# Low parts of weight units made by a transfer that adds, in the attention of a two-layer trunk

## The chip, the core and the metric

The kernel runs on one core of a Trainium2 chip. A core has TensorE (matrix products into the PSUM banks), VectorE, ScalarE and GpSimd (elementwise work), SyncE (here only a queue for transfers), an on-chip memory SBUF of 128 partitions, and 16 DMA engines that carry transfers between HBM and SBUF. Each engine works through its own queue in order and waits on semaphores. The metric is the device time of one execution, in microseconds, as the median of several runs.

## What is computed

The reference is a decoder trunk with two layers on 512 positions of width 1024, in float32. Layer 0 mixes tokens by a gated MLP, layer 1 by attention with 16 heads of 64, each followed by a gated MLP with a causal convolution of three taps. The change lies in the attention:

```python
proj = h @ w_qkvf
q, k, v, f_logit = jnp.split(proj, [D_MODEL, 2 * D_MODEL, 3 * D_MODEL], axis=-1)
log_f = jax.nn.log_sigmoid((f_logit + b_f).astype(jnp.float32))
cum = jnp.cumsum(log_f, axis=1).transpose(0, 2, 1)
...
logits = logits + cum[:, :, q0:q1, None] - cum[:, :, None, :q1]
p = jax.nn.softmax(jnp.where(mask, logits, neg), axis=-1)
o = jnp.einsum("bhqk,bkhd->bqhd", p, vb)      # per block of 128 queries
return o @ w_o
```

## The kernel before

All weights are cut into 176 units of 128x1024 float32 (512 KB), used once each, in order. `fetch` (line 75) brings in one unit: SyncE issues its transfer to a `raw` buffer (three of them), ScalarE casts `raw` to the high part `whi`, rounded to the type TensorE takes at speed, and VectorE subtracts that from `raw` to make the low part `wlo` (`split`, line 110). `whi` and `wlo` have two buffers each, so the cast for unit n+1 waits until TensorE is through with unit n-1. `unit` (line 85) fetches one unit ahead of the one that it returns. Each product is three matmuls (`triple`, line 164): L167 high by high, L168, and L169. Where the weight is the stationary operand, as in the attention's products, L167 and L168 read `whi` and only L169 reads `wlo`.

The attention (`fox`, line 363) first makes v (units 96 to 103), then q and k, two units for each pair of heads (units 104 to 119), and the output product (units 120 to 127; the first three of them are first halves of three groups of outputs, 120 to 122). The products of q, k and the output come from a generator that is woven with the attention proper: 20 triples run first, and then each of 71 slots takes two triples and one step of `attend`. A unit has eight triples, so it lasts four slots, one head. In a slot, `logits` (line 561) makes the logits of one block of queries, of 128 to 512 columns, in one of two PSUM banks `s` by three matmuls (L572 to L574), takes the row maximum on VectorE (L576), the exponential on ScalarE (L578), and normalises on VectorE (L579, L580). `turn` (line 582) transposes the probabilities of an earlier slot (L590) and splits them in two (`hl`, by `split`), and `values` (line 596) multiplies them by v (L602, L603). After the last triple of q or k, `stack_q` and `stack_k` scale the product and split it into the stacked operands of the logits (L528 to L534, L540 to L546), on VectorE and ScalarE; one cast of each is on GpSimd, and it issues no transfers.

The kernel names the engine of every instruction, but not its place in the queue: the framework plans the order of each queue from dependences, the order in which the kernel is written, and estimated durations. It may put an instruction ahead of one that is written earlier.

Of the kernel before, what the change touches and what calls it, by code (L numbers as in the profile page):

```python
# [8 lines left out]
F32 = mybir.dt.float32  # L9
F32R = mybir.dt.float32r  # L10
BF16 = mybir.dt.bfloat16
I32 = mybir.dt.int32
AF = mybir.ActivationFunctionType
ALU = mybir.AluOpType
# [28 lines left out]
class Trunk:  # L43
# [28 lines left out]
        return self.ps(tag)  # L72


    def fetch(self):
        nc = self.nc
        raw = self.sb("raw", 3, [P, 1024])
        nc.sync.dma_start(out=raw, in_=self.ins["w"][self.iu])
        self.iu += 1
        hi = self.sb("whi", 2, [P, 1024], F32R)  # L80
        lo = self.sb("wlo", 2, [P, 1024], F32R)
        self.split(hi, lo, raw)
        self.ahead.append((hi, lo))

    def unit(self, depth=2):
# [752 lines left out]
```

## Time and profile before

| | us |
|---|---|
| median of 3 runs (1090.64 to 1091.21) | 1091.2 |
| the profiled execution | 1091.33 |
| its span, first to last instruction | 1089.6 |
| TensorE busy | 1074.4 (99%) |
| VectorE busy | 622.1 (57%) |
| ScalarE busy | 441.5 (41%) |
| GpSimd busy | 70.4 (6%) |

The profile shows one execution. Busy time on TensorE includes overlap of matmuls in flight, so 99% doesn't say that it works at its best rate; its waits are read from the distance between starts of instructions. The products of q, k and the output, with the attention slots between them, lie between 605 and about 807 us of the span. The granted clock of TensorE is 0.994 of full speed over the whole.

### The profile page before, as it was taken

Reading aid. Unit: us, or ns where it says so; the run is one execution under the profiler, and the core shown is the slowest. Engines: PE = TensorE matmul, PEld = TensorE weight load, DVE = VectorE, ACT = ScalarE, POOL = GpSimd, SP = SyncE. Lnnn points to the kernel's source line nnn. Section 1 sums busy time; section 2 is a strip of 40 time slices with the busy share of each in tenths; the row PEclk is TensorE's granted clock in tenths of the full one; section 3 lists DMA queues with packets and bytes.
Section 4 is the critical chain, followed back from the end, with each engine's and each line's share of the span. In section 5 each row is a group of like instructions: output and inputs, shape, how many; then the busy total and the mean of one; then the engine's idle time right before and its main releaser. Section 6 shows DMA issues by size and latency. Waiting matters only on the chain.

```text
span 1089.6 us, 12928 instructions
## 1 busy us (share of the span) xinstructions
PE 1074.4 (99%) x5018; PEld 885.5 (81%) x5018; DVE 622.1 (57%) x1007; ACT 441.5 (41%) x706; POOL 70.4 (6%) x62
## 2 busy tenths in 40 slices
PE   8999999999999999999999999999989999999997
PEld 7878888888888888888887888877768888888886
DVE  5535856534555665545254699999564655655242
ACT  6332333322333433333133577777442433433232
POOL 5000000001200000001020010110030000000000
PEclk9999999999999999999999999999989999999999
DMA  6222222222223222222222211111122223232222
GB/s 257 96 79 96 93 82 78 96 98 96 98 78 97 97 97 97 99 96 98 97 96 83 98 61 41 60 62 59 59 78 97 95 97 98 78 116 78 97 97 78
DMA packets 28669, 99.44 MB, mean 91 GB/s; under 512 B 3456, under 2 KB 3712, under 8 KB 28608
## 3 DMA queue, kind: packets, MB, share of 16 engines
q1 hardware_dynamic: 27744, 96.42, 25.7%
q10 hardware_dynamic: 864, 2.20, 0.5%
q8 instruction: 39, 0.64, 0.2%
q14 instruction: 22, 0.18, 0.1%
HBM read 96.12 MB, written 2.10 MB: 90 GB/s over the span
## 4 chain that ended last, share of the span: by engine, by line
PE 89%; DVE 7%; ACT 2%; DMA 1%; issue 1%; ACTq 0%; DVEq 0%
PE psg L167 11%; PE psg L168 11%; PE psg L169 11%; PE pss L169 9%; PE pss L167 9%; PE pss L168 9%; PE psa L167 4%; PE psa L168 4%; PE psa L169 4%; PE psb L167 4%; PE psb L168 4%; PE psb L169 4%; DVE wlo L113 2%; DVE hl L113 1%; DVE z L545 1%; PE psa L590 1%
## 5 line engine op out<-in xcount | busy, mean ns | idle before, releaser
L113 DVE TENSOR_TENSOR wlo<-raw,whi 128x1024 fp32r<-128x1024 f32 (+1 forms) x173 | 219.6, 1269 | 371.4 <-ACT whi L112 359.2
L112 ACT CAST whi<-raw 128x1024 fp32r<-128x1024 f32 (+1 forms) x173 | 180.8, 1045 | 453.0 <-PE psg L168 132.2
L167 PE MATMUL psg<-x,whi 128*128 128x512 f32 x336 | 136.1, 405 | 0.0
L169 PE MATMUL psg<-x,wlo 128*128 128x512 f32 x336 | 131.3, 391 | 0.0
L168 PE MATMUL psg<-x,whi 128*128 128x512 f32 x336 | 130.9, 390 | 0.0
L167 PE MATMUL pss<-x,whi 128*128 128x512 f32 x192 | 75.9, 395 | 0.0
L168 PE MATMUL pss<-x,whi 128*128 128x512 f32 x192 | 74.7, 389 | 0.0
L169 PE MATMUL pss<-x,wlo 128*128 128x512 f32 x192 | 74.7, 389 | 0.0
L169 PEld LDWEIGHTS psg<-x,wlo 128*128 128x128 f32 x336 | 63.1, 188 | 13.5
L167 PEld LDWEIGHTS psg<-x,whi 128*128 128x128 f32 x336 | 63.9, 190 | 11.1
L141 POOL TENSOR_TENSOR tmp<-tmp,tmp 128x512 f32<-128x512 f32 x28 | 47.0, 1678 | 399.8 <-ACT tmp L140 398.5
L168 PEld LDWEIGHTS psg<-x,whi 128*128 128x128 f32 x336 | 63.3, 188 | 11.2
L167 PE MATMUL psg<-z,whi 128*128 128x512 f32 x128 | 50.3, 394 | 0.6 <-ACT z L112 0.6
L169 PE MATMUL psg<-z,wlo 128*128 128x512 f32 x128 | 50.0, 391 | 0.0
L168 PE MATMUL psg<-z,whi 128*128 128x512 f32 x128 | 49.8, 389 | 0.0
L169 PE MATMUL pss<-z,wlo 128*128 128x512 f32 x112 | 44.8, 402 | 3.7 <-DVE wlo L113 3.7
L167 PE MATMUL psa<-x,whi 128*128 128x512 f32 x120 | 47.3, 394 | 0.0
L169 PE MATMUL psa<-x,wlo 128*128 128x512 f32 x120 | 46.7, 389 | 0.0
L168 PE MATMUL psa<-x,whi 128*128 128x512 f32 x120 | 46.7, 389 | 0.0
L167 PE MATMUL psb<-x,whi 128*128 128x512 f32 x120 | 46.7, 389 | 0.0
L169 PE MATMUL psb<-x,wlo 128*128 128x512 f32 x120 | 46.7, 389 | 0.0
L168 PE MATMUL psb<-x,whi 128*128 128x512 f32 x120 | 46.7, 389 | 0.0
(282 smaller groups left out, 2221.7 us busy)
## 6 DMA issues: line engine op xcount, KB each, us to landing
raw<-w SPq DMA_DIRECT2D x175, 512.0 KB
out<-v SPq DMA_DIRECT2D x8, 256.0 KB
h<-x ACTq DMA_DIRECT2D x3, 512.0 KB
raw<-w SPq DMA_DIRECT2D x2, 256.0 KB
h<-x ACTq DMA_DIRECT2D x2, 256.0 KB
pt<-ws SPq DMA_DIRECT2D x1, 512.0 KB
pt<-bs SPq DMA_DIRECT2D x1, 512.0 KB
z<-cum SPq DMA_DIRECT2D x32, 8.0 KB
```

The source lines that it names most:

```text
L112: nc.scalar.copy(out=hi, in_=src)
L113: nc.vector.tensor_tensor(out=lo, in0=src, in1=hi.bitcast(F32), op=ALU.subtract)
L141: nc.gpsimd.tensor_tensor(out=self.acc, in0=self.acc, in1=sq, op=ALU.add)
L167: self.nc.tensor.matmul(out, ah, bh, start=start, stop=False)
L168: self.nc.tensor.matmul(out, ah, bl, start=False, stop=False)
L169: self.nc.tensor.matmul(out, al, bh, start=False, stop=stop)
L545: nc.vector.tensor_tensor(out=bk[0:HD], in0=f[own], in1=ak[own].bitcast(F32), op=ALU.subtract)
L590: nc.tensor.transpose(pt[:, (qi - kb) * P : (qi - kb + 1) * P], pr[:, o : o + P], self.ident)
```

## The change

Only `fetch` is changed. For units 106 to 122 (the units of q and k from the second pair of heads on, and the first three of the output product) VectorE's subtraction is gone. In its place ScalarE writes the negated high part into `lo`, and GpSimd issues a transfer that reads the unit again from HBM and adds it onto what stands in `lo`: `lo` becomes the unit less its high part. All other units are split as before.

```diff
+    ADDED = range(106, 123)
+
     def fetch(self):
         nc = self.nc
         raw = self.sb("raw", 3, [P, 1024])
         nc.sync.dma_start(out=raw, in_=self.ins["w"][self.iu])
-        self.iu += 1
         hi = self.sb("whi", 2, [P, 1024], F32R)
         lo = self.sb("wlo", 2, [P, 1024], F32R)
-        self.split(hi, lo, raw)
+        if self.iu in self.ADDED:
+            nc.scalar.copy(out=hi, in_=raw)
+            nc.scalar.activation(out=lo, in_=hi.bitcast(F32), func=AF.Copy, scale=-1.0)
+            nc.gpsimd.dma_start(out=lo, in_=self.ins["w"][self.iu].bitcast(F32R), accum_op=ALU.add)
+        else:
+            self.split(hi, lo, raw)
+        self.iu += 1
         self.ahead.append((hi, lo))
```

## Rows read from the trace of the kernel before

**Rows 1.** The page, busy us, share of the span and count, by engine.
```profile
PE 1074.4 (99%) x5018; PEld 885.5 (81%) x5018; DVE 622.1 (57%) x1007; ACT 441.5 (41%) x706; POOL 70.4 (6%) x62
```

**Rows 2.** Windows: stretch, its length, busy us by engine, clock, DMA share, GB/s.
```profile
680.00:700.00 20.00, 19.79 (x111) 16.05 (x110) 18.91 (x44) 15.07 (x37) 2.23 (x2) 1.00 0.17 55
...
780.00:800.00 20.00, 15.70 (x65) 11.25 (x64) 12.80 (x16) 10.42 (x17) 4.53 (x3) 0.92 0.13 45
```

**Rows 3.** TensorE in order of time: start, us, engine, line, operation [idle before].
```profile
692.97 0.38 PE L590 MATMUL psa<-ident,pt 128*128 128x128 f32 x2
693.56 0.50 PE L572 MATMUL pss<-z,z 128*128 128x512 f32 x1 [0.21 <-ACT pt L578]
...
699.30 0.40 PE L169 MATMUL psg<-x,wlo 128*128 128x512 f32 x1
...
703.08 0.38 PE L590 MATMUL psa<-ident,pt 128*128 128x128 f32 x2
703.22 0.48 PE L572 MATMUL pss<-z,z 128*128 128x512 f32 x1
```

**Rows 4.** Waits, 620 to 800 us: us in total, times, longest.
```profile
PEld pss L572 <- ACT pt L578: 3.4, 8, 0.5
```

**Rows 5.** The chain that ended last, 600 to 820 us: start, us, what.
```profile
649.05 1.67 DVE wlo L113
...
688.72 1.21 DVE wlo L113
...
692.57 0.34 DVE sm L576
692.94 0.57 ACT pt L578 x2
```

**Rows 6.** The tile raw, 600 to 800 us: count, duration ns min/median/max.
```profile
L112 ACT CAST whi<-raw x23: 1027/1048/1056, 599.8 to 797.4; 128x1024 fp32r<-128x1024 f32 x23
L113 DVE TENSOR_TENSOR wlo<-raw,whi x22: 1212/1225/2296, 600.9 to 795.5; 128x1024 fp32r<-128x1024 f32 x22
```

**Rows 7.** ScalarE in order of time, from 687 us.
```profile
687.61 1.05 ACT L112 CAST whi<-raw 128x1024 fp32r<-128x1024 f32 x1 [0.67 <-PE psg L168]
...
688.92 0.61 ACT L544 CAST z<-tmp 64x512 fp32r<-64x512 f32 x1
...
692.05 0.48 ACT L112 CAST hl<-psa 128x384 fp32r<-128x384 f32 x1
692.94 0.47 ACT L578 ACTIVATE pt<-pss,sm 128x256 f32<-128x256 f32 x1 [0.41 <-DVE sm L576]
```

**Rows 8.** SyncE's queue in order of time, one issue of a unit.
```profile
700.57 0.33 SPq L78 DMA_DIRECT2D raw<-w  x1
```

**Rows 9.** Windows of 0.5 us behind that issue, first and last with data.
```profile
701.50:702.00 0.50, 0.50 (x4) 0.41 (x3) 0.50 (x2) 0.18 (x1) 0.00 (x0) 1.00 0.88 221
...
703.00:703.50 0.50, 0.50 (x5) 0.41 (x3) 0.50 (x2) 0.35 (x1) 0.00 (x0) 1.00 0.24 90
```

**Rows 10.** GpSimd in order of time, two casts of one size.
```profile
649.03 0.61 POOL L546 CAST z<-tmp 64x512 fp32r<-64x512 f32 x1 [3.58 <-DVE tmp L540]
...
688.78 1.61 POOL L546 CAST z<-tmp 64x512 fp32r<-64x512 f32 x1 [4.16 <-DVE tmp L540]
```

**Rows 11.** ScalarE in order of time, casts of units 106 and 107.
```profile
610.43 1.05 ACT L112 CAST whi<-raw 128x1024 fp32r<-128x1024 f32 x1 [3.58 <-PE psg L168]
...
615.91 1.05 ACT L112 CAST whi<-raw 128x1024 fp32r<-128x1024 f32 x1
```

**Rows 12.** TensorE in order of time: first reads of wlo, units 106, 107, 125.
```profile
616.35 0.39 PE L169 MATMUL psg<-x,wlo 128*128 128x512 f32 x1
...
622.49 0.39 PE L169 MATMUL psg<-x,wlo 128*128 128x512 f32 x1
...
797.84 0.80 PE L169 MATMUL pss<-z,wlo 128*128 128x512 f32 x1 [3.68 <-DVE wlo L113]
```

**Rows 13.** VectorE in order of time, the widest normalisation.
```profile
697.70 0.48 DVE L580 TENSOR_SCALAR pt<-pt,sm 128x512 f32<-128x512 f32 x1
```

## The prediction, on record before the change was run

> **What bounds the kernel now.** I read five views, from coarse to fine. The page's busy times come first: TensorE is busy in 1074.4 of 1089.6 us, VectorE in 622.1 and ScalarE in 441.5 [rows 1]. So only what makes TensorE wait can be won, and the averages of the other engines say nothing until they are cut by stage. The windows by stage do that: in the attention VectorE is busy in 18.91 of 20 us, ScalarE in 15.07, GpSimd in 2.23, and the DMA engines are used to 0.17; in the last stretch before the next layer TensorE is busy in only 15.70 of 20 [rows 2]. The reader is to see there that VectorE, idle in nearly half of the whole span, is almost full just where the change takes work from it. Whether TensorE pays for that is seen in the order of its instructions. Between the two transposes and the 512-wide logits of a slot there are 0.59 us at 692.97, but 0.14 us at 703.08, one unit later [rows 3]. The same two steps without a wait are worth 0.14, so this wait costs 0.45 us. In the waits of the stretch from 620 to 800 us, that line's weight load waits for the exponential 8 times, 3.4 us in all [rows 4]; six of the eight are the 0.45 kind, one for each pair of heads in the steady part. The chain of waits says what is behind it: the subtraction that makes `wlo` at 688.72, then VectorE's queue up to the row maximum at 692.57, the exponential at 692.94, and TensorE at 693.56 [rows 5]. The logits may not start until the exponential has emptied the bank used two slots before.
>
> So attention is bound by TensorE with a small loss, 3.4 us, that VectorE's queue causes. That is the most the change can win at the place where it acts, 0.3% of the time.
>
> **The change part by part.** *Removed:* 17 subtractions on VectorE, 1.225 us each [rows 6], 20.8 us; two of them per 20 us bring VectorE from 18.9 to 16.5. None lies on TensorE itself. At 688.72 the subtraction stands in front of the maximum that the stalled logits wait for; with it gone that maximum can be done up to 1.2 us sooner, more than the 0.45 us that TensorE waits. Bounds: 0 (another link holds the exponential) and 3.4 us; I take 3.4, since 1.2 is well over 0.45.
>
> *Added on ScalarE:* 17 negations of 128x1024. The trace has no such operation; the nearest row is the cast of the same size on the same engine, 1.048 us [rows 6]. That is 17.8 us, and 15.07 becomes 17.2 of 20 us. ScalarE has room on average, but not everywhere: from the cast of `whi` at 687.61 it runs without a gap to 692.53 (the last cast starts at 692.05 and takes 0.48) [rows 7], and the exponential starts 0.41 us after that. A negation right behind `whi` would push the exponential to about 693.5, 0.55 us later than now. The order on a queue is not the order in which the kernel is written: `whi` is written behind the casts of `k`, and runs ahead of them (the first is at 688.92). A planner orders by what it takes to be ready. With VectorE free at 688.7 the maximum is ready early, so I expect its exponential to be put ahead of the casts of the next slot, and the negation into the gaps. I count 0, with bounds of 0 and +0.55 us per pair.
>
> *Added on GpSimd and the DMA engines:* 17 transfers of 512 KB that read the unit a second time and add. Nothing in the trace adds in flight, so I bound it. Below: the plain transfer of the same unit is issued at 700.57; data moves from 701.5 to 703.1, which is 2.6 us from issue to the last byte, 1.6 of it data [rows 8, 9]. Above: four times the data time, and an issue on GpSimd as long as that engine's longest cast, 1.61 us [rows 10]: 0.95 + 6.4 + 1.6 = 9.0 us. I take twice the data time, since both operands must be read, and a short issue of 0.6: 0.95 + 3.2 + 0.6 = 4.75 us. A sentence apart: the Trainium skill ("DMA: Bandwidth & Descriptors", section on the anatomy of one DMA on the gpsimd path) gives 2.0 us and the bytes over 436 GB/s, by which an estimate for this transfer is 3.2 us, 4.4 if the bytes count twice; no row here shows it.
>
> What this wait covers: `whi` starts at 687.61 [rows 7], and the first matmul that reads the new `lo` is at 699.30 [rows 3], 11.7 us later. Take off the cast and the negation, 1.05 each: 9.6 us are left if the negation is prompt. If it is put behind ScalarE's run without gaps (3.9 us later, less the 0.5 saved by what it no longer pushes), 6.2 are left. 4.75 fits both; 9.0 fits the first alone. Behind the issue on GpSimd's queue stand only the two casts per pair of heads, which feed logits of the next pair: they have many us.
>
> *The first units.* Unit 106 is fetched before attention slots stretch the units. Its `whi` starts at 610.43 [rows 11] and TensorE wants `lo` at 616.35 [rows 12]: 5.9 us, less 2.1 for cast and negation, leaves 3.8. With 4.75 TensorE waits 0.95 us; by the bounds 0 to 5.2. The `whi` of unit 107 starts at 615.91 and its `lo` is wanted at 622.49, 0.95 later by then: 6.6 + 0.95 - 2.1 = 5.4, so no second wait; with 9.0 the first wait has already moved it. From unit 108 on the slots give the time above.
>
> *At nothing:* the raw buffer comes free after the cast instead of after the subtraction, so SyncE's next transfer starts about 1.2 us sooner and may overlap the adding one; with the DMA engines at 0.17, and two more transfers of some 3.2 us in 20, they stay near half used. The wait of 3.68 us at 797.84 [rows 12], with the low clock behind it, is for unit 125, whose `lo` VectorE still makes: 0 either way, unless the planner's order there shifts.
>
> *A rule against the change.* In this trace GpSimd and VectorE slow each other: the cast of `ak` takes 1.61 us at 688.78, beside `wlo`, and 0.61 at 649.03 [rows 10], where instead `wlo` took 1.67 [rows 5] against 1.225. The Trainium skill ("SBUF — State Buffer", section "Who interferes with whom") says that VectorE in its two-port modes (the normalisation's kind of instruction can enter them) and GpSimd lock each other out of a shared port pair, whoever issues first, and that descriptor generation on GpSimd needs it. The trace agrees for casts; none shows it for a transfer. What a hold between the two would cost, from rows: four normalisations per unit, of 0.48 us and less [rows 13], under 1.9 us together, can delay an issue, or an issue of 0.6 to 1.6 us can hold VectorE. The first is at most 0.5 above the 6.2 - 4.75 = 1.45 us left in the worse order, and the second is about the 1.2 us taken from VectorE; both come back below as rivals.
>
> *Sum:* -3.4 + 0.95 = -2.45 us. The profiled execution took 1091.33 us (span 1089.6), 0.13 above the median of 1091.2: 1088.9 against it, 1088.8 against the median.
>
> **Rivals.**
> 1. *The late low part (slower).* The adding transfer takes longer than the room left, and TensorE waits at the third matmul of a unit. It decides from 6.2 us if the negation is late, 9.6 if it is prompt. For: the room is estimated from an order that the planner will make anew, and nothing shows the adding rate. Against: DMA engines at 0.17 and 11.7 us of cover. At 7.5 us with a late negation: 1.3 us for each of 7 pairs, 9.1, and 3.7 for unit 106, less the 3.4 won if all stalls still go: +9.4, 1100.6. A hold by all four normalisations, 1.9 us more on 4.75, gives 6.65: 7 x 0.45 + 2.85 - 3.4 = +2.6, 1093.8.
> 2. *ScalarE takes VectorE's place (slower).* The negation stands in the run without gaps, and the exponential comes 0.55 us later in each of 7 pairs: +3.85 and 0.95 = +4.8, 1096.0. For: that run is dense, and ScalarE's casts feed VectorE's. Against: with VectorE earlier, the exponential can go ahead of casts that now stand before it.
> 3. *Nothing moves.* The wait at the 512-wide logits stays, since the casts of `k` and not the subtraction hold the maximum, and only the start costs: +0.95, 1092.1; or it goes and a start of 3.4 eats it: 1091.2.
> 4. *It doesn't free VectorE.* Issues hold VectorE as long as the subtraction did. For: the casts above. Against: the longest of them cost VectorE 0.45 us (1.67 against 1.225), not 1.2. The time is that of rival 3.
>
> **How the numbers follow.** Forecast 0.44; late low part 0.20; ScalarE 0.12; nothing moves, by rivals 3 and 4 together, 0.24. What a measurement of this kernel can tell from no change is 0.2%, 2.2 us: faster is below 1089.0, slower above 1093.4. The forecast lies at the edge: its own range, with a start of 0 to 2 us, is 1087.8 to 1089.8. Of its 0.44, 0.36 is under 1089.0; another 0.06 for a planner's order that also shortens the late wait of 3.68 us or loses the small ones at the end: faster 0.42. Slower takes most of rival 1 (0.16) and rival 2 (0.11), 0.27; the rest, 0.31, is the same. The range goes from 1086.5 (all stalls gone, no start, and about 1 us of the tail) to 1097.0 (rival 2 and the lighter half of rival 1).
>
> **What would show it.** In the changed profile: no wait of the 512-wide logits on the exponential (right), or one still there of 0.45 (rival 3) or about 1.0 (rival 2); VectorE near 16.5 of 20 us in the attention; ScalarE near 17.2; a wait of about 1 us at the third matmul of unit 106, and none in later units. Waits of the `lo` matmuls in each unit mean rival 1. The prediction is wrong if the time leaves the range, or if the time fits but the 3.4 us are still there and something else moved.

## The result, and the profile after

The changed kernel takes 1097.91 us (median of 5 runs, 1097.19 to 1099.75), the kernel before, run beside it, 1091.2 us (5 runs, 1090.47 to 1091.84). The ratio is 1.0066, with a 95% interval of 1.0052 to 1.0081: slower by 0.5 to 0.8%. The forecast was 1088.8 us and its range ended at 1097.0, so the time lies 0.9 us outside, and the direction is the wrong one.

The profiled execution of the changed kernel took 1099.12 us, with a span of 1097.4, 7.8 us more than before. All lines of `split` and behind it stand seven lines further down than before; new are L84 (the cast to `whi`), L85 (the negation into `wlo`) and L86 (the adding transfer).

The page, busy time by engine, and its lines of the two queues that carry units (packets, MB, share of the 16 engines' span):

```profile
PE 1075.5 (98%) x5018; PEld 885.7 (81%) x5018; DVE 605.5 (55%) x990; ACT 457.0 (42%) x723; POOL 77.7 (7%) x79
...
q1 hardware_dynamic: 27744, 96.42, 25.4%
q0 software_dynamic: 2448, 8.91, 4.7%
```

Beside [rows 1] VectorE lost 17 instructions and 16.6 us, ScalarE gained 17 and 15.5 us, GpSimd 17. The change does what it says. TensorE has the same work, 5018 instructions and 1.1 us more of busy time, in a span 7.8 us longer: it waits more. Where, the windows show (length, busy us of PE, PEld, DVE, ACT and POOL, granted clock, DMA share, GB/s):

```profile
619.50:623.00 3.50, 3.50 (x10) 2.70 (x10) 0.69 (x1) 1.73 (x2) 0.00 (x0) 0.53 0.95 183
...
680.00:700.00 20.00, 19.01 (x107) 15.31 (x106) 16.09 (x41) 16.02 (x36) 2.72 (x4) 1.00 0.47 108
```

Against 680:700 of [rows 2], VectorE fell from 18.91 to 16.09 of 20 us, ScalarE rose from 15.07 to 16.02, and TensorE fell from 19.79 to 19.01. The engine that had been nearly full is freer, no engine has become full, and TensorE does less. The first line is a second place, at the start of the attention, where TensorE runs without a gap at a granted clock of 0.53.

**The start.** TensorE in order of time (start, us, line, operation, idle before and what ended it):

```profile
616.24 0.39 PE L175 MATMUL psg<-x,whi 128*128 128x512 f32 x1
618.53 0.50 PE L176 MATMUL psg<-x,wlo 128*128 128x512 f32 x1 [1.90 <-DMA wlo<-w]
...
620.26 0.63 PE L176 MATMUL psg<-x,wlo 128*128 128x512 f32 x1
620.69 0.63 PE L174 MATMUL psg<-x,whi 128*128 128x512 f32 x1
```

The third matmul of unit 106 starts 2.29 us after the one before it, where such neighbours are otherwise 0.23 apart: a wait of 2.06 us for the adding transfer. Behind it the distance grows to 0.43 us (620.26 to 620.69), which is the lower of the two clock levels, 1.2 instead of 2.4 GHz, for about nine matmuls. Against the kernel before, TensorE is 0.12 us late ahead of the wait (616.24, where its row has 616.12) and 3.93 late behind this stretch (625.59 against 621.66 at the first 256-wide logits). So in this execution the start costs 3.8 us: 2.06 of waiting, and 1.7 that go with the low clock.

**The steady part.** TensorE again, two units of one pair of heads:

```profile
713.92 0.49 PE L597 MATMUL psa<-ident,pt 128*128 128x128 f32 x3
714.71 0.33 PE L597 MATMUL psa<-ident,pt 128*128 128x128 f32 x1 [0.30 <-DVE pt L587]
714.81 0.35 PE L579 MATMUL pss<-z,z 128*128 128x256 f32 x1
...
719.50 0.38 PE L597 MATMUL psa<-ident,pt 128*128 128x128 f32 x2
719.63 0.48 PE L579 MATMUL pss<-z,z 128*128 128x512 f32 x1
...
724.06 0.49 PE L597 MATMUL psa<-ident,pt 128*128 128x128 f32 x3
725.26 0.33 PE L597 MATMUL psa<-ident,pt 128*128 128x128 f32 x1 [0.71 <-DVE pt L587]
725.36 0.35 PE L579 MATMUL pss<-z,z 128*128 128x256 f32 x1
```

The wait of [rows 3] is gone: between two transposes and the 512-wide logits there are 0.13 us. A new one stands two slots later: the last of the four transposes of a head's 512-wide block comes apart from the other three. It waits for the normalisation (L587), that is for the end of the chain maximum, exponential, sum, normalisation of those same logits. The waits from 620 to 800 us have one line for it (us in total, times, longest), in the place of the line in [rows 4]:

```profile
PEld psa L597 <- DVE pt L587: 8.7, 12, 0.9
```

One number sums up the steady part: the time from the 256-wide logits of a head to those of the same head in the next pair. Before it was 19.78 us, now it is 20.7 (704.66, in the row not shown, to 725.36). Over six pairs that is about 5.4 us, of which some 0.5 come back at both ends of the attention: when TensorE reaches the wait for unit 125 it is 8.8 us late, 4.9 more than behind the start.

**The chain** in that stretch (start, us, what) says why the normalisation is late:

```profile
717.52 0.59 ACT hl L119
718.13 0.56 ACT pt L585 x2
718.69 0.83 ACT wlo L85
719.67 0.59 ACT tmp L618
720.28 0.69 DVE tmp L619
721.00 0.56 DVE hl L120
...
722.00 0.68 DVE z L120
722.68 0.34 DVE hl L120
723.02 0.61 DVE sm L583
723.65 0.79 ACT pt L585 x2
```

Two things are to be read here. ScalarE runs without a gap from 714.65 to 722.11, and the negation (L85) stands in the middle of that run, in front of the copy (L618) for which VectorE waits. And VectorE, late by then, takes two splits (`z` and `hl`, 722.00 and 722.68) before the maximum (L583) of the 512-wide logits, although TensorE had finished these at about 720.4 (the last of them, the mask, started at 720.19). In the kernel before, the same two splits stood ahead of that maximum in this unit of a pair, too:

```profile
694.91 0.41 DVE L113 TENSOR_TENSOR hl<-psa,hl 128x256 fp32r<-128x256 f32 x1
695.24 0.68 DVE L113 TENSOR_TENSOR z<-tmp,z 128x512 fp32r<-128x512 f32 x1
...
695.92 0.67 DVE L576 TENSOR_REDUCE sm<-pss 128x1 f32<-128x512 f32 x1
```

There its logits were complete at about 694.37 (the mask started at 694.14), so the maximum came 1.55 us later, and the fourth transpose did not wait. In the changed kernel it comes 2.5 us after its logits: the normalisation of the 384-wide block (721.66) now stands ahead of it as well, and VectorE idles for ScalarE. In the other unit of a pair it came 0.04 us after its logits and now comes 2.0 after them, behind that normalisation and two splits. VectorE's own rows in the changed kernel show it idle for ScalarE ahead of these splits:

```profile
717.52 0.69 DVE L552 TENSOR_TENSOR z<-tmp,z 64x512 fp32r<-64x512 f32 x1 [0.60 <-ACT z L551]
...
720.28 0.69 DVE L619 TENSOR_TENSOR tmp<-psb,tmp 64x512 f32<-64x512 f32 x1 [0.56 <-ACT tmp L618]
```

**The tail** has the same wait for unit 125 as in [rows 12], 3.68 us, 8.8 us later. Behind it fewer matmuls run at the low clock, which gives back about 1.0 us; that the change is the reason is not shown.

```profile
806.63 0.50 PE L176 MATMUL pss<-z,wlo 128*128 128x512 f32 x1 [3.68 <-DVE wlo L120]
```

Start +3.8, steady part +4.9, tail -1.0, and the 0.1 from before the start: +7.8 us, as between the spans.

### The profile page after: what moved, and what is told of

It reads as the page before. It is cut to its first block, busy times and chain, and to the rows that moved or that the text cites. A ratio compares the mean times of both kernels' runs of the same rounds, so it can differ in the third digit from the quotient of the medians.

```text
span 1097.4 us, 12948 instructions
## 1 busy us (share of the span) xinstructions
PE 1075.5 (98%) x5018; PEld 885.7 (81%) x5018; DVE 605.5 (55%) x990; ACT 457.0 (42%) x723; POOL 77.7 (7%) x79
## 4 chain that ended last, share of the span: by engine, by line
PE 84%; DVE 6%; ACT 6%; issue 2%; DMA 1%; ACTq 0%; DVEq 0%
PE psg L174 10%; PE psg L175 10%; PE psg L176 10%; PE pss L176 9%; PE pss L175 9%; PE pss L174 9%; PE psa L174 4%; PE psa L175 4%; PE psa L176 4%; PE psb L174 4%; PE psb L176 4%; PE psb L175 4%; ACT pt L585 2%; DVE sm L583 1%; ACT wlo L85 1%
## 5 line engine op out<-in xcount | busy, mean ns | idle before, releaser
L120 DVE TENSOR_TENSOR wlo<-raw,whi 128x1024 fp32r<-128x1024 f32 (+1 forms) x156 | 198.7, 1274 | 365.2 <-ACT whi L119 353.1
L119 ACT CAST whi<-raw 128x1024 fp32r<-128x1024 f32 (+1 forms) x156 | 163.1, 1045 | 443.6 <-PE psg L175 124.5
```

The lines of the kernel that those rows point to most:

```text
L119: nc.scalar.copy(out=hi, in_=src)
L120: nc.vector.tensor_tensor(out=lo, in0=src, in1=hi.bitcast(F32), op=ALU.subtract)
```

## The experiments

After the result two things might make the time: the start (the transfer of the first unit, with the clock behind it) and the negation on ScalarE. A rival to the second was that the transfers themselves disturb the attention. A third, the order in which VectorE's queue takes the maximum, is a rival in experiments 2 and 4; these left a wait that neither engine's load explains, and so 5 to 7 try it by itself. All kernels are compared with runs of the kernel before on the same chip. The first four ran together, the last three too.

**1. Start the change two units later.**

```diff
-    ADDED = range(106, 123)
+    ADDED = range(108, 123)
```

> The range starts at unit 108 instead of 106, so VectorE splits the two units that are fetched before the attention slots. In the changed kernel TensorE waits 2.06 us for the low part of unit 106 and then runs nine matmuls at the low clock, 0.2 us more each, with the ends of that stretch about 2.1 us. Theory A (the start costs 4.2 us, wait and clock together): 1093.7 us, and no low clock between 615 and 625 us. Rival (the clock falls at that place for another reason): only the wait goes, 1095.8. Rival (the start is not a cost of its own, since the next waits take it up): 1097.9. In all of them the waits of the transposes on the normalisation, 0.86 and 0.46 us for each pair of heads, stay.

Measured: 1095.31 us (5 runs, 1094.81 to 1096.51), ratio 1.0045 (1.0031 to 1.0058). The window of the start, with the full clock and no gap of TensorE:

```profile
605.00:620.00 15.00, 15.00 (x68) 12.44 (x67) 8.94 (x11) 7.91 (x11) 2.15 (x2) 1.00 0.26 77
```

The start's loss is gone, wait and low clock together, and the steady part is the same, 20.67 us per pair. The two profiled executions differ by 3.8 us (1099.12 to 1095.31), which is what the trace gave for the start; the expectation's 4.2 was too much. The medians differ by 2.6 us, which is nearer to the wait alone, 2.06; the time lies between theory A's 1093.7 and the first rival's 1095.8, and the clock of 1.00 speaks against that rival's reason. How many matmuls run at the low clock in a usual execution stays open: only one run of the changed kernel has a trace, and its mean granted clock, 0.994, is the lowest of the five (the others have 0.996 or 0.997).

**2. A short negation, and a transfer that writes instead of adding.**

```diff
-            nc.scalar.activation(out=lo, in_=hi.bitcast(F32), func=AF.Copy, scale=-1.0)
-            nc.gpsimd.dma_start(out=lo, in_=..., accum_op=ALU.add)
+            nc.scalar.activation(out=lo[:, 0:64], in_=hi[:, 0:64].bitcast(F32), func=AF.Copy, scale=-1.0)
+            nc.gpsimd.dma_start(out=lo, in_=...)
```

> ScalarE negates 64 columns of each unit instead of 1024, and the transfer writes the unit instead of adding it; queue order, bytes read from HBM and the wait of the transfer on the negation are as in the changed kernel, and VectorE's order differs in one place. It leaves out the low part: what stands there is the unit itself. Theory B (the waits of 0.86 and 0.46 us per pair come from ScalarE's 1.05 us per unit, in a stretch in which it has no room): they go, 7.5 us in all, and the low part of unit 106 comes about 0.9 us sooner: 1086.5 to 1089.5 us. Rival C (they come from the order that the planner now gives VectorE, which puts the maximum of the 512-wide logits behind a split): the order is the same, so they stay, 1094 to 1097.

Measured: 1091.06 us (11 runs, 1090.51 to 1092.87), ratio 1.0004 (0.9995 to 1.0013). The number of instructions and nearly their order on each queue are those of the changed kernel; ScalarE's time is less, 0.26 us a negation instead of 1.06, and so is the transfer's, which experiment 3 shows to cost the steady part nothing. That brings most pairs from 20.7 to 19.7 us (one of them takes 20.05). The time lies between the forecasts of theory B and of rival C, so neither holds alone. What is left is a small wait of the fourth transpose, in one unit of each pair:

```profile
698.76 0.33 PE L597 MATMUL psa<-ident,pt 128*128 128x128 f32 x1 [0.17 <-DVE pt L587]
698.85 0.36 PE L579 MATMUL pss<-z,z 128*128 128x256 f32 x1
```

VectorE's rows before it, in the same kernel:

```profile
695.50 0.68 DVE L120 TENSOR_TENSOR z<-tmp,z 128x512 fp32r<-128x512 f32 x1
696.10 0.42 DVE L120 TENSOR_TENSOR hl<-psa,hl 128x256 fp32r<-128x256 f32 x1
696.44 0.68 DVE L583 TENSOR_REDUCE sm<-pss 128x1 f32<-128x512 f32 x1
```

The 512-wide logits were complete at about 694.4 (the mask of them started at 694.23). Their maximum could have been taken then, and comes 2.0 us later, behind two splits, and the normalisation ahead of these, that nobody waits for so urgently. So the negation's time on ScalarE is most of the loss, and the queue's order is a second part that is there without it.

**3. The negation without the transfer.**

```diff
             nc.scalar.activation(out=lo, in_=hi.bitcast(F32), func=AF.Copy, scale=-1.0)
-            nc.gpsimd.dma_start(out=lo, in_=..., accum_op=ALU.add)
```

> The negation as in the changed kernel, but no transfer that adds. It leaves out that addition: the low part is the negated high part. Theory B (ScalarE): the waits of 0.86 and 0.46 us per pair stay, and only the start's 4.2 us go, 1093.7 us. Rival D (the transfers disturb the attention: their issues hold VectorE off its port, or their data slows SBUF): the waits go as well, 1086 to 1088. Theory A is tested here too: without a transfer nothing is late at unit 106.

Measured: 1095.31 us (5 runs, 1095.13 to 1095.87), ratio 1.0043 (1.0031 to 1.0056), 20.66 us per pair. The line of the waits (one line number lower in this kernel) is that of the changed kernel:

```profile
PEld psa L596 <- DVE pt L586: 8.6, 12, 0.9
```

Time and waits are those of experiment 1 (the 1093.7 expected took 4.2 us off for the start). So the transfers, their issues on GpSimd and their traffic cost nothing in the steady part, and all of the loss there comes with the negation and the order. The start is free here too, since nothing waits for a transfer.

**4. The negation on GpSimd**, from unit 108 on.

```diff
-            nc.scalar.activation(out=lo, in_=hi.bitcast(F32), func=AF.Copy, scale=-1.0)
+            nc.gpsimd.tensor_scalar(out=lo, in0=hi.bitcast(F32), scalar1=-1.0, scalar2=None, op0=ALU.mult)
```

> GpSimd negates instead of ScalarE, from unit 108 on; the transfer adds as in the changed kernel, so nothing is left out. Theory B (ScalarE): the waits of the transposes on the normalisation go and the start is gone, 1086 to 1087 us, provided that GpSimd's negation takes under about 4 us and the low parts land in time. Rival C (planner's order on VectorE, which is nearly that of the changed kernel): 1093.7. Rival D (GpSimd's work holds VectorE): VectorE's normalisations and splits get longer beside the negation, and TensorE waits again, 1090 or more.

Measured: 1092.58 us (11 runs, 1091.53 to 1093.78), ratio 1.0017 (1.0008 to 1.0026), against 1.0045 with the same units on ScalarE. The pair takes 19.87 us instead of 20.67, so the negation on ScalarE costs 0.80 us per pair. GpSimd takes much longer for it (tile `wlo`, min/median/max in ns), and the late landing costs a wait at the first changed unit:

```profile
L85 POOL TENSOR_SCALAR wlo<-whi x15: 2762/2768/3244, 623.3 to 761.1; 128x1024 fp32r<-128x1024 f32 x15
```

By distance that wait is 1.25 us; 6 x 0.09 for the pairs is another 0.5. Together 1.8, where the ratio says 0.9 to 2.8. In the steady part this kernel has neither a negation on ScalarE nor a subtraction on VectorE, and it is still no faster than before: the maximum comes 2.15 and 1.54 us after its logits. Rival D has a small part: beside GpSimd's negation some of VectorE's splits of 64x512 take 0.86 us instead of 0.69. The measured time lies between the forecasts of B and C here too. So the order had to be tried alone.

**5 and 6. The maximum first, with and without the change.** The planner prefers an instruction written in this block to others of its queue. In 5 the change starts at unit 108; 6 is the kernel before and this edit, nothing else.

```diff
-        nc.vector.tensor_reduce(out=nm, in_=s[:, 0:w], axis=AX.X, op=ALU.max, negate=True)
+        with self.tc.high_priority():
+            nc.vector.tensor_reduce(out=nm, in_=s[:, 0:w], axis=AX.X, op=ALU.max, negate=True)
```

> The changed kernel from unit 108 on, and the row maximum of the logits is given a higher priority, so that the planner puts it ahead of the splits; nothing else is edited. Where the 512-wide maximum stood behind the split of the output (0.68 us) and a split of the probabilities (0.42), it is now ahead of them; in the other unit of a pair it is ahead of a split of q (0.69). Theory E (ScalarE's extra microsecond only shows because the maximum stands behind work that nobody waits for): the waits of 0.86 and 0.46 us per pair go, 7.4 us, 1088 us. Rival B (ScalarE simply has no room there, whatever the order): under 2 us is won, 1093.5 to 1095.3. Between them: the 0.46 goes and the 0.86 shrinks by less than half, 1091 to 1092.

> The kernel before with the same priority for the row maximum, and no unit taken from VectorE. Theory F (the waits that the prediction wanted to win, 0.45 us per pair at the 512-wide logits, are a matter of order on VectorE and not of its load): they go, about 3 us, 1088 us. Rival G (VectorE, full to 18.9 of 20 us, is the cause): they stay or move to another place, 1090 to 1092.

Measured, 5: 1089.53 us (11 runs, 1088.83 to 1090.0), ratio 0.9989 (0.998 to 0.9998). Measured, 6: 1087.37 us (5 runs, 1086.14 to 1087.65), ratio 0.9966 (0.9954 to 0.9979), faster than both kernels. The window of 6, its VectorE and its TensorE:

```profile
680.00:700.00 20.00, 20.00 (x114) 16.44 (x113) 18.95 (x46) 15.66 (x37) 2.15 (x2) 1.00 0.20 62
```

```profile
693.15 0.67 DVE L577 TENSOR_REDUCE sm<-pss 128x1 f32<-128x512 f32 x1
693.74 0.68 DVE L113 TENSOR_TENSOR z<-tmp,z 128x512 fp32r<-128x512 f32 x1
```

```profile
696.08 0.60 PE L591 MATMUL psa<-ident,pt 128*128 128x128 f32 x4
696.44 0.36 PE L572 MATMUL pss<-z,z 128*128 128x256 f32 x1
```

VectorE is as full as ever, 18.95 of 20 us, with all its subtractions; the maximum now runs ahead of the split of `z`, 0.74 us after its logits (0.29 in the other unit of a pair); the four transposes come in one piece, and TensorE is busy in 20.00 of 20. Its list of waits from 620 to 800 us has no line for the logits or for the normalisation. So the wait of [rows 4] came not from how much VectorE had to do, but from what it did first. The edit puts all maxima ahead, and other instructions of the queue move with them; which single move counts most was not tried apart.

In 5 most of the loss is gone too (1089.53 lies between the 1088 of theory E and the 1091 to 1092 of the middle case), but the pair still takes 0.40 us more than in 6, six times 2.4 where the medians differ by 2.2. Its waits from 620 to 800 us keep two small kinds, the normalisation, and now the transfer, which the faster units want sooner:

```profile
PEld psa L598 <- DVE pt L588: 1.6, 6, 0.4
...
PEld psg L176 <- DMA wlo<-w: 1.3, 4, 0.6
```

That is what the change costs with a good order, once its start is left out.

**7. The maximum first, and the subtraction off VectorE without loading ScalarE:** the negation on GpSimd as in 4, from unit 110 on, and the edit of 5.

> GpSimd negates, from unit 110 on (unit 108 was 1.25 us late when GpSimd negated it), and the maximum has the higher priority. ScalarE has its load of before and VectorE is free of the subtraction. Theory E and F together: no steady wait is left, 1088 us, and not faster than the kernel before with the priority alone, so taking the subtraction off VectorE brings nothing by itself. Rival G (VectorE's load matters too): 1 us or more below that kernel.

Measured: 1087.53 us (7 runs, 1086.86 to 1089.24), ratio 0.9968 (0.9957 to 0.998). It cannot be told from experiment 6, though VectorE has more room; TensorE is busy in 20.00 of 20 in both windows, so hardly a wait is left to win:

```profile
680.00:700.00 20.00, 20.00 (x113) 16.40 (x112) 17.33 (x42) 15.09 (x37) 8.87 (x7) 1.00 0.50 108
```

**All kernels side by side**, us from the 256-wide logits of a head to those of the same head in the next pair, read from TensorE's order in each trace, and the ratio to before:

| negation | VectorE's order as planned | maximum first |
|---|---|---|
| none (subtraction on VectorE) | 19.78; 1 | 19.28; 0.9966 (6) |
| on ScalarE, from unit 108 | 20.67; 1.0045 (1) | 19.68; 0.9989 (5) |
| on GpSimd | 19.87; 1.0017 (4) | 19.33; 0.9968 (7) |
| on ScalarE, 64 of 1024 columns | 19.7; 1.0004 (2) | not run |

For 7 it is the distance from 698 us on; the pair before that has a wait of 0.23 at the first changed unit. In each row the order is worth 0.5 to 1.0 us per pair. In each column the negation on ScalarE costs 0.4 to 0.9, and taking the subtraction off VectorE wins 0.1 at most. No run takes the subtraction off and keeps the order of before.

## Why the prediction was wrong

**The step that failed** is "I take 3.4, since 1.2 is well over 0.45". It counted the wait at the 512-wide logits as won and put nothing in its place. The waits in question did go, as forecast, but the 3.4 us were not won: in the planner's new queue the maximum of the 512-wide logits starts later behind them than before, behind a normalisation in one unit of a pair and behind that and two splits in the other, and the wait came back at their transposes. With neither the subtraction nor ScalarE's negation (experiment 4) the pairs cost 0.5 us more than before instead of 3.4 less. Experiment 6 wins those us with every subtraction in place, and 7 shows that removing them adds nothing to that. I asked of the stall what it waited behind, and saw the subtraction in [rows 5]; I did not ask whether the instructions in front of the maximum had to be there at all.

**The second**, and the larger one by size, is ScalarE's negation, "I count 0, with bounds of 0 and +0.55 us per pair". Its duration was right (1.056 us against the 1.05 of the cast); its place was not. It was expected in the gaps, and stands inside the run without gaps (718.59), ahead of a copy that VectorE waits for. With the planned order it costs 0.80 us per pair (20.67 against 19.87), 4.8 in six, with the maximum first 0.35 to 0.40 (19.68 against 19.28 and 19.33): above the bound in the first case. The bound was the shift of one exponential. Its working was also a little short: 692.53 and 1.05 make 693.58, which is 0.64 later and not 0.55. What it left out is that VectorE, idle for ScalarE's copy (0.56 at 720.28), hands its delay on to its own maximum; the idle time of 0.60 at 717.52 is no part of this, since experiment 2 has it too.

**The third** is the first unit, "With 4.75 TensorE waits 0.95 us", and no term for the clock. Measured were 2.06 us, inside the bounds of 0 to 5.2, and 1.7 more with the low clock. The terms, in the tile `wlo` and in ScalarE's and GpSimd's rows: `whi` starts at 610.55, the negation at 611.63, the transfer is issued at 613.03, 0.34 after the negation's end, and the matmul starts at 618.53. That is 8.0 us instead of the 6.9 that the working gives.

```profile
L85 ACT ACTIVATE wlo<-whi x17: 1046/1056/1072, 611.6 to 768.0; 128x1024 fp32r<-128x1024 f32 x17
L86 POOL DMA_DIRECT2D wlo<-w x17: 840/855/1006, 613.0 to 769.5; - x17
...
DMA to landing us min/median/max: 5.0/5.2/5.5
```

**What held.** The transfer lands 5.2 us after its issue, 4.75 were taken. The estimate worked out from the Trainium skill ("DMA: Bandwidth & Descriptors", section on the anatomy of one DMA on the gpsimd path), 4.4 us with the bytes counted twice, is below the shortest landing, 5.0; the measurement decides. Unit 107 and the later units have no wait for a transfer in the changed kernel (rival 1 holds for the start alone). DMA engines are at 0.47 ("near half used"), and the transfers cost the steady part nothing (3 against 1). VectorE's 16.1 was forecast as 16.5, ScalarE's 16.0 as 17.2, in a window that holds less of the work, since a pair takes 20.7 us. The wait for unit 125 stayed at 3.68. GpSimd's casts, 1.61 us beside the subtraction in [rows 10], are back at 0.61 without it:

```profile
715.62 0.61 POOL L553 CAST z<-tmp 64x512 fp32r<-64x512 f32 x1 [4.64 <-DVE tmp L547]
```

**The rivals.** Rival 2, ScalarE in VectorE's place, had the mechanism and 12 in 100. Its mark was a longer wait of the 512-wide logits; those lost theirs, and the fourth transposes got one instead. Its price was 0.55 us per pair where the whole change cost 0.89, and with 0.95 for the start it came to 1096.0 (1096.6 with 0.64). Both the missing order and the missing clock made it too small. "What would show it" looked for waits at the 512-wide logits and at the `lo` matmuls only: one at the transposes was not on the list, though it was the result.

## What to carry to other kernels

Where one engine waits for a result of a nearly full one, look first at what stands ahead of that result in the full engine's queue; putting one kind of instruction first can win what taking away another doesn't. Work that moves to an engine with room on average is paid at the place in that engine's queue where it lands, so read that engine's gapless runs, and who waits for what stands behind them, before calling it free. Where an automatic planner orders the queues, a change of the instructions can make a new order, and a time should be forecast with that as its own term.

## What the runs showed of the hardware

An adding transfer costs the DMA engines about 1.7 times a plain one. Its queue's 4.7% of 16 engines' 1097.4 us, over 17 transfers, is 3.03 us each; in experiment 2 the queue of GpSimd's 17 plain writes has 2.8% of 1088.8 us, 1.79 each. From issue to landing it takes 5.2 us, a plain write by GpSimd of the same size 4.3 (experiment 2, median), and its issue occupies GpSimd for 0.855 us against 0.53.

The clock fell after one wait of 2.06 us in a stretch that was otherwise dense, to a granted 0.53 in the 3.5 us shown above, and the 1.7 us lost then were nearly as much as the wait.

GpSimd's negation of 128x1024 takes 2.77 us where ScalarE's takes 1.06, and still the pair is shorter with it here (19.87 against 20.67 us). And a normalisation of VectorE beside a cast of GpSimd took 0.56 us, alone 0.42; the cast of that moment (710.36) is ahead of both:

```profile
710.36 0.62 POOL L541 CAST z<-tmp 64x512 fp32r<-64x512 f32 x1 [2.12 <-DVE tmp L535]
```

```profile
710.63 0.56 DVE L587 TENSOR_SCALAR pt<-pt,sm 128x384 f32<-128x384 f32 x1
...
721.66 0.42 DVE L587 TENSOR_SCALAR pt<-pt,sm 128x384 f32<-128x384 f32 x1
```

The Trainium skill ("SBUF — State Buffer", section "Who interferes with whom") says that VectorE in its two-port modes, which such a normalisation can enter, and GpSimd lock each other out of a shared port pair for a whole instruction, and that a VectorE instruction with two inputs in SBUF, such as the subtraction, contends with one of GpSimd that reads SBUF. The cast's 1.61 us and its return to 0.61 agree with the second; the prediction set them beside the first. These rows agree with the first in part: normalisation and cast overlap by 0.35 us, and the normalisation is only 0.14 longer. Its other half, that GpSimd's issue of a transfer needs the same ports, shows no cost here: with the transfers left out (experiment 3) the time is the same.
